# A two-layer encoder trunk on one core: when the attention layer's gated products are issued, and where two sums stand in their engines' order

## The chip, the core and the metric

The kernel runs on one core of a Trainium2 chip. The core has five engines that work side by side, each on its own list of instructions in a fixed order: TensorE (PE: matrix products and transposes into PSUM), VectorE (DVE), ScalarE (ACT), GpSimd (POOL) and SyncE (SP, here only a queue for DMAs). Engines wait for each other by semaphores, and an instruction that waits holds up everything behind it on its own engine. POOL's list holds DMAs too. The metric is the device time of one execution in microseconds.

## The reference, cut to what matters

512 tokens and 16 meta tokens (T = 528), width 2048, two layers. Layer 0 is grouped-query attention with 16 query heads in 8 groups of two, each group with one key and one value head; layer 1 is gated linear attention. For layer 0:

```python
proj = h @ w_in
q, k, v, gate = jnp.split(proj, ...)
q = apply_axial_rope(rmsnorm(q, q_norm), ang_row, ang_col)
k = apply_axial_rope(rmsnorm(k, k_norm), ang_row, ang_col)
s = jnp.einsum('bqkgd,bskd->bkgqs', qb, k) * (ATTN_HEAD_DIM ** -0.5)
p = jax.nn.softmax(s, axis=-1)
o = jnp.einsum('bkgqs,bskd->bqkgd', p, v)
return (o * jax.nn.silu(gate)) @ w_out
```

The change concerns the product `o * silu(gate)`, the mean of squares in `rmsnorm` of q and k, and how the large weight products (`h @ w_in`, `@ w_out`, and layer 1's `h @ w_in`) are formed.

## The kernel before, in words

**Numbers in two parts.** Every fp32 operand of a product is split into a high part, rounded by ACT (`A.copy`, line 132), and a rest, subtracted by DVE (line 133): `uh`, `ul` for activations, `whi`, `wlo` for weights (three buffers of each, used in turn). Each product is three matmuls: high by high, high by rest, rest by high.

**What sets the order.** The program is traced by Python. `Clock` (line 39) is the author's planner: each product step advances it by an estimated cost in microseconds, `clk.after(dt, fn)` puts work `dt` later, and `clk.drive` runs a generator that yields its own pauses. So the planner's due times decide in which order instructions are traced. A scheduler then builds each engine's list from priorities (`tc.high_priority(n)` moves work ahead) and from when it thinks the operands are there; work that seems ready can float ahead of what was traced before it. `pin` (`keep_in_program_order`) forbids that for one instruction: it stays behind the instruction traced last before it on the same engine. It adds no semaphore.

**The attention stage** (lines 796 to 818) goes through eight groups. In group g, PE runs the three projections of group g+1 (`qkv`: k, then two q heads), and between their steps the planner sets the attention of group g: nine tiles of queries, each with `softmax` (products L701 to L703 into `s`; maximum L706 on DVE; exponential L709 on ACT) and, one slot later, `transposed`: PE transposes the probabilities `pn` into PSUM tiles `pT` and `pTm` (L721, L723), ACT and DVE split them into `ph`, `pl`, `pmt` (L725 to L728). `pT` and `pTm` come from a PSUM pool of two buffers, so a tile's transposes must wait until the tile before has been split. The fifth tile holds the 16 meta tokens of both heads and is split in two halves, one for each head. A projection ends in `rope`: POOL sends four DMAs (L314) that swap rows, waits for them, and runs three tensor operations (`rotate`, L315 to L317); ACT and DVE split the squares, PE sums them with a matrix of ones (L328, L329), DVE scales (L331), ACT makes the inverse root (L136, L137), DVE multiplies (L335).

**The gated products** of the group before, two heads of each, run beside this in `stored_gates` (line 652). The gate values were stored earlier and are loaded by `load_gates`. `begin` scales them (L658, DVE) and forms SiLU (L140 to L142 on ACT, L689 on POOL); `inverse` loads the softmax denominators' inverses, spread over all partitions (L641, POOL's queue); `end` runs on POOL alone: `divided` (L645 and a narrow L646), the product with the attention output (L664) and its store (L665). By the planner: begin of head 0 at 7.0, its `inverse` at 9.2, begin of head 1 at 10.0, its `inverse` and the end of head 0 at 18.0, the end of head 1 at 21.2.

**The paired weight products**, `seven` (line 217), form two column blocks of a weight matrix in seven products instead of eight, from sums of the four quarter blocks a11, a12, a21, a22. It runs eight times ahead of the attention, four times in the output projection, and six times in layer 1's projection. In each run `parts` splits the weights of seven products in the order w1, w6, w2, s, a21, a11, a22, two products ahead of their use, as buffers come free; DVE forms four sums (L234). The first, s = a21 + a22, with priority 90, may be issued as soon as its two loads have landed.

Of the kernel before, what the change touches and what calls it, by code (L numbers as in the profile page):

```python
# [14 lines left out]
ALU = mybir.AluOpType  # L15
# [67 lines left out]
def hybrid_encoder(  # L83
# [6 lines left out]
    V, A, G, PE = nc.vector, nc.scalar, nc.gpsimd, nc.tensor  # L90
    clk = Clock()
    pin = tc.keep_in_program_order
# [26 lines left out]
    ones_r = const.tile([P, P], F32R, name="ones_r")  # L119
# [11 lines left out]
    def split(hi, lo, src):  # L131
        A.copy(hi, src)  # L132
        V.tensor_tensor(lo, src, hi.bitcast(F32), op=ALU.subtract)  # L133

    def rsqrt_inplace(t):
        A.activation(t, t, AF.Ln)  # L136
        A.activation(t, t, AF.Exp, scale=-0.5)  # L137
# [79 lines left out]
    def seven(src, c, ys, th, tl, free, ps_x):  # L217

        def quarter(t, i, j):
            with tc.high_priority(AHEAD + 200):  # L220
                nc.sync.dma_start(out=t.rearrange("p (k n) -> p k n", n=P),
                                  in_=src[:, j * KH:(j + 1) * KH, c + i * P:c + (i + 1) * P])
            return t

        def parts(raw):
            with tc.high_priority(AHEAD):
                hi = wpool.tile([P, 1024], F32R, tag="whi", name="whi")
                lo = wpool.tile([P, 1024], F32R, tag="wlo", name="wlo")
                split(hi, lo, raw)
            return [t.rearrange("p (k n) -> p k n", n=P) for t in (hi, lo)]  # L230

        def sums(o, a, b, op=ALU.subtract):
            with tc.high_priority(90):
                V.tensor_tensor(o, a, b, op=op)  # L234

        def product(w, b, ps=None, more=False):
            if ps is None:
                ps = ps_x.tile([P, 512], F32, tag="x", name="px")[:, :HALF]
            bh, bl = b
            for k in range(KH):  # L240
                PE.matmul(ps, w[0][:, k], bh[:, k], start=k == 0 and not more, stop=False, skip_group_check=more)  # L241
                PE.matmul(ps, w[0][:, k], bl[:, k], start=False, stop=False, skip_group_check=more)  # L242
                PE.matmul(ps, w[1][:, k], bh[:, k], start=False, stop=k == KH - 1,  # L243
                          skip_group_check=more)
                clk.step(3 * (HALF + 7) / 2400)
            return ps

        def add(o, ps, y):
            with tc.high_priority(AHEAD + 100):
                V.tensor_tensor(o, ps, y, op=ALU.add)  # L250

        def of_u(j, n):
            a, b = HALVES[n]
            return [t[:, j * KH:(j + 1) * KH, a:b] for t in (uh, ul)]

        def of_t(o):
            return [t[:, :, o:o + HALF] for t in (th, tl)]
        a11, a21, a22, s, a12, spare = free
        for t, i, j in ((a11, 0, 0), (a12, 0, 1), (a21, 1, 0), (a22, 1, 1)):
            quarter(t, i, j)  # L260
        y1, y2 = ys
        l, r = slice(0, HALF), slice(HALF, T)
        w1 = parts(a11)
        w6 = parts(a12)
        sums(s, a21, a22, ALU.add)
        sums(a21, a11, a21)
        sums(a11, s, a11)
        w2 = parts(a11)
        p1 = ps_p.tile([P, 512], F32, tag="pp", name="pp")[:, :HALF]
        product(w1, of_u(0, 0), p1)  # L270
        A.copy(y1[:, l], p1)
        add(y1[:, l], product(w6, of_u(1, 0)), y1[:, l])
        product(w2, of_t(T2), p1, True)
        A.copy(y1[:, r], p1)
        p5 = product(parts(s), of_t(T1))
        A.copy(y2[:, r], p5)
        sums(a11, a12, a11)
        product(parts(a21), of_t(T3), p1, True)
        A.copy(y2[:, l], p1)
        add(y2[:, r], y2[:, l], y2[:, r])  # L280
        product(parts(a11), of_u(1, 1), p5, True)
        add(y1[:, r], p5, y1[:, r])
        product(parts(a22), of_t(T4), p1, True)
        A.copy(y2[:, l], p1)
        return [spare, a21, a12, a11, s, a22]
# [33 lines left out]
    def rope(qw, sq, outs, steps):  # L319
        rotate(qw, wk.tile([P, T], F32, tag="qs", name="qs"))  # L320
        sh = wk.tile([P, T], F32R, tag="sh", name="sh", bufs=1)
        sl = wk.tile([P, T], F32R, tag="sl", name="sl", bufs=1)
        split(sh, sl, sq)
        f = sq

        def sums(a, b):
            ps = ps_p.tile([P, 512], F32, tag="pp", name="ssq")[:, :b - a]
            PE.matmul(ps, ones_r, sh[:, a:b], start=True, stop=False)  # L328
            PE.matmul(ps, ones_r, sl[:, a:b], start=False, stop=True)  # L329
            with tc.high_priority(AHEAD):  # L330
                V.scalar_tensor_tensor(f[:, a:b], ps, 1.0 / P, erow[:, a:b], op0=ALU.mult, op1=ALU.add)  # L331

        def late():
            rsqrt_inplace(f)
            V.tensor_tensor(qw, qw, f, op=ALU.mult)  # L335
            for hi, lo, a, b in outs:
                split(hi, lo, qw[:, a:b])
        for step, part in zip(steps, HALVES):
            clk.after(step, lambda part=part: sums(*part))
        clk.after(steps[2], late)  # L340
# [62 lines left out]
    for i, (si, off) in enumerate(((0, 0), (1, 0), (1, P))):  # L403
        for j, (a, b) in enumerate(HALVES):
            n = 2 * i + j
            if n < 3:
                ps = ps_p.tile([P, 512], F32, tag="pp", name="pp")
            else:
                ps = ps_g.tile([P, 512], F32, name=f"g{n}")
            ps = ps[:, :b - a]  # L410
# [140 lines left out]
    for h in range(3):  # L551
        y = yp.tile([P, T], F32, tag=f"y{h % 2}", name="y")
# [6 lines left out]
    y = yp.tile([P, T], F32, tag="y1", name="y")  # L559
# [91 lines left out]

    def stored_gates(hs, held):

        grs = ready.pop() if ready else load_gates(hs)
        gss = []

        def begin(i):
            pin(V.tensor_tensor(grs[i], grs[i], rrow, op=ALU.mult))  # L658
            gss.append(silu(grs[i]))

        def end(i):
            divided(gss[i], grs[i])
            og = held[hs[i] % 2]
            G.tensor_tensor(og, og, gss[i], op=ALU.mult)  # L664
            nc.gpsimd.dma_start(out=og_d[hs[i]], in_=og)  # L665
        yield 7.0
        for i, (x, y) in enumerate(((2.2, 0.8), (8.0, 0.0))[:len(hs)]):
            begin(i)
            yield x
            inverse(hs[i], grs[i])  # L670
            yield y
        for i in range(len(hs)):
            end(i)
            yield 3.2
        if hs and hs[-1] < 12:
            ready.append(load_gates([h for h in (hs[-1] + 1, hs[-1] + 2) if h < 13]))

    ready = []

    def load_gates(hs):  # L680
        grs = [wa.tile([P, T], F32, tag="gr", name="gr") for _ in hs]
        for gr, h in zip(grs, hs):
            pin(nc.gpsimd.dma_start(out=gr, in_=g_d[h]))
        return grs

    def silu(gr):
        gs = wa.tile([P, T], F32, tag="gs", name="gs", bufs=2)
        sigmoid(gs, gr)
        pin(G.tensor_tensor(gs, gs, gr, op=ALU.mult))  # L689
        return gs  # L690
# [102 lines left out]

    qk, vv = qks[0][0], values(0)
    held = None
    for g in range(KV):
        o_sb = o_tiles()
        if g == KV - 1:
            clk.after(10.5, make_sel)
        att = clk.drive(chain(iter([3.0]), attention(g, qk, vv, o_sb, SLOTS[g])))  # L800
        gates = [] if g == 0 else [2 * g - 2, 2 * g - 1]
        stored = clk.drive(stored_gates([h for h in gates if h < 13], held))
        if g + 1 < KV:
            nxt = qkv(g + 1)
        for h in gates:
            if h < 13:
                continue
            gs = gate(h)
            rb = wa.tile([P, T], F32, tag="gr", name="rb")
            inverse(h, rb)  # L810
            divided(gs, rb)
            og = held[h % 2]
            G.tensor_tensor(og, og, gs, op=ALU.mult)
            nc.gpsimd.dma_start(out=og_d[h], in_=og)
        if g + 1 < KV:
            clk.finish(att, stored)
            qk, vv = nxt
            held = o_sb
# [28 lines left out]
    for m in range(2):  # L847
        for j, (a, b) in enumerate(HALVES):
            ps = (ps_t.tile([P, 512], F32, tag="t", name="po") if m and j else
                  ps_p.tile([P, 512], F32, tag="pp", name="pp"))[:, :b - a]  # L850
# [42 lines left out]
    for m in range(2, 5):  # L893
        y = y_tile(m % 2)
# [19 lines left out]
    hs = [tp.tile([P, T], F32, name=f"h{k}") for k in range(KT)]  # L914
# [51 lines left out]
    for i in range(2):  # L966
        for a, b in HALVES:
            ps = ps_g.tile([P, 512], F32, name=f"g{i}{a}")[:, :b - a]
# [116 lines left out]
    for a, b in HALVES:  # L1085
        ps = ps_t.tile([P, 512], F32, tag="t", name="lrf")[:64, :b - a]
# [406 lines left out]
    y = [fp.tile([P, D], F32, name=f"y{t}") for t in range(4)]  # L1493
# [75 lines left out]
```

## Time and profile before

| | |
|---|---|
| Median of 3 runs | 1774.61 us (1770.96 to 1779.83) |
| The profiled execution | 1778.32 us, its span 1776.4 us |
| PE busy | 1737.5 us, 98% of the span |
| DVE, ACT, POOL busy | 1153.0, 1000.4, 386.9 us |
| Attention stage | about 297 to 750 us of the span |
| Runs of `seven` | about 116 to 286, 806 to 890, 1020 to 1150 us |

The span reaches from the first to the last instruction. PE's granted clock was 0.999 of full speed. A row of the timeline has the start in us from the beginning of the span, the duration in us, engine, line, operation, written tile <- read tiles, and in brackets how long the engine sat idle before, and for whom. In a table of waits, a row has who waited for whom, the total in us, how often, and the longest.

### The profile page before, as it was taken

How to read it: one execution, taken by the hardware profiler on the slowest of the kernel's cores; microseconds unless marked ns; L12 is line 12 of the kernel's file. 1: busy time of each engine (PE TensorE's matmuls, PEld its weight loads, DVE VectorE, ACT ScalarE, POOL GpSimd, SP SyncE). 2: the span in 40 equal slices, each digit the busy share in tenths (PEclk: the TensorE clock that was granted, in tenths of full speed). 3: DMA queues.
4: the chain of work that ended last, by engine and by line, in shares of the span. 5: the costliest groups of instructions: out<-in, count | busy, mean ns of one | idle time of the engine just before them, and what ended most of it. 6: DMA issues, size and time to landing. Idle time of an engine off the chain costs nothing.

```text
span 1776.4 us, 31587 instructions
## 1 busy us (share of the span) xinstructions
PE 1737.5 (98%) x12427; PEld 1635.0 (92%) x12427; DVE 1153.0 (65%) x1791; ACT 1000.4 (56%) x2056; POOL 386.9 (22%) x492
## 2 busy tenths in 40 slices
PE   8999999999999999999999999999999999999998
PEld 8999999999999999999999899998898989888886
DVE  5767875566566666786766976567685865863224
ACT  5545445666666666644457454577684765853222
POOL 3103301356456645231141001110100000000000
PEclk9999999999999999999999999999999999999999
DMA  7444434233333334464485344343342432344323
GB/s 244 142 133 132 130 118 125 79 110 109 85 106 103 107 85 127 133 200 119 121 249 173 104 135 120 110 136 90 87 111 73 114 87 86 107 141 174 95 95 130
DMA packets 272387, 218.80 MB, mean 123 GB/s; under 512 B 13196, under 2 KB 243280, under 8 KB 271712
## 3 DMA queue, kind: packets, MB, share of 16 engines
q1 hardware_dynamic: 253200, 157.41, 31.4%
q0 software_dynamic: 19040, 59.40, 10.1%
q8 instruction: 97, 1.59, 0.4%
q14 instruction: 50, 0.41, 0.1%
HBM read 176.83 MB, written 33.44 MB: 118 GB/s over the span
## 4 chain that ended last, share of the span: by engine, by line
PE 77%; issue 7%; DVE 7%; ACT 5%; DMA 2%; POOL 2%; SPq 0%; DVEq 0%; POOLq 0%; ACTq 0%
PE pp L155 12%; PE pp L157 12%; PE pp L156 12%; PE pp L241 3%; PE pp L242 3%; PE pp L243 3%; PE f L1481 2%; PE f L1479 2%; PE f L1480 2%; PE px L243 2%; PE px L241 2%; PE px L242 2%; DVE wlo L133 2%; ACT whi L132 2%; PE pT L721 1%
## 5 line engine op out<-in xcount | busy, mean ns | idle before, releaser
L155 PE MATMUL pp<-uh,whi 128*128 128x264 f32 (+1 forms) x1872 | 585.4, 313 | 0.7 <-ACT y L888 0.5
L157 PE MATMUL pp<-uh,wlo 128*128 128x264 f32 (+1 forms) x1872 | 576.3, 308 | 1.4 <-DVE wlo L133 1.1
L156 PE MATMUL pp<-ul,whi 128*128 128x264 f32 (+1 forms) x1872 | 575.3, 307 | 0.0
L133 DVE TENSOR_TENSOR wlo<-wraw,whi 128x1024 fp32r<-128x1024 f32 (+1 forms) x226 | 287.9, 1274 | 238.4 <-ACT whi L132 237.9
L132 ACT CAST whi<-wraw 128x1024 fp32r<-128x1024 f32 (+1 forms) x226 | 235.4, 1042 | 261.3 <-PE f L1481 83.4
L157 PEld LDWEIGHTS pp<-uh,wlo 128*128 128x128 f32 x1872 | 353.4, 189 | 18.8 <-DVE wlo L133 1.6
L155 PEld LDWEIGHTS pp<-uh,whi 128*128 128x128 f32 x1872 | 353.4, 189 | 16.9 <-ACT y L888 0.7
L156 PEld LDWEIGHTS pp<-ul,whi 128*128 128x128 f32 x1872 | 353.8, 189 | 13.5
L132 ACT CAST whi<-x 128x1024 fp32r<-128x1024 f32 x72 | 75.5, 1049 | 104.9 <-PE pp L242 52.1
L133 DVE TENSOR_TENSOR wlo<-x,whi 128x1024 fp32r<-128x1024 f32 x72 | 90.2, 1260 | 40.0 <-ACT whi L132 39.7
L709 ACT ACTIVATE pn<-s,mx 128x528 f32<-128x528 f32 (+1 forms) x72 | 50.5, 701 | 71.3 <-DVE mx L706 71.3
L706 DVE TENSOR_REDUCE mx<-s 128x1 f32<-128x528 f32 (+1 forms) x72 | 50.8, 706 | 52.8 <-PE s L703 52.3
L243 PE MATMUL px<-uh,wlo 128*128 128x264 f32 x288 | 82.0, 285 | 0.8 <-DVE wlo L133 0.8
L241 PE MATMUL px<-uh,whi 128*128 128x264 f32 x288 | 82.2, 285 | 0.4 <-ACT whi L132 0.4
L242 PE MATMUL px<-ul,whi 128*128 128x264 f32 x288 | 81.5, 283 | 0.0
L1481 PE MATMUL f<-whi,ul 128*128 128x512 f32 x192 | 75.6, 394 | 0.0
L1479 PE MATMUL f<-whi,uh 128*128 128x512 f32 x192 | 75.5, 393 | 0.0
L1480 PE MATMUL f<-wlo,uh 128*128 128x512 f32 x192 | 75.3, 392 | 0.0
L314 POOL DMA_DIRECT2D qs<-qw x96 | 48.0, 506 | 95.1 <-ACT sq L308 72.9
L726 DVE TENSOR_TENSOR pl<-pT,ph 128x512 fp32r<-128x512 f32 (+1 forms) x80 | 47.6, 595 | 26.7 <-ACT ph L725 26.2
L243 PE MATMUL pp<-t0h,wlo 128*128 128x264 f32 x192 | 54.4, 283 | 2.1 <-DVE wlo L133 2.1
L243 PEld LDWEIGHTS px<-uh,wlo 128*128 128x128 f32 x288 | 54.1, 188 | 1.0 <-DVE wlo L133 1.0
(488 smaller groups left out, 4433.9 us busy)
## 6 DMA issues: line engine op xcount, KB each, us to landing
wraw<-in_gla_w_in_dram SPq DMA_DIRECT2D x82, 512.0 KB, 3.9
wraw<-in_attn_w_in_dram SPq DMA_DIRECT2D x75, 512.0 KB, 4.0
wraw<-in_gla_w_out_dram SPq DMA_DIRECT2D x32, 512.0 KB, 3.9
wraw<-in_attn_w_out_dram SPq DMA_DIRECT2D x23, 512.0 KB, 4.5
x<-in_attn_w_in_dram SPq DMA_DIRECT2D x19, 512.0 KB, 4.4
x<-in_gla_w_in_dram SPq DMA_DIRECT2D x14, 512.0 KB, 4.5
qs<-qw POOLq DMA_DIRECT2D x96, 66.0 KB, 3.3
g_d<-y POOLq DMA_DIRECT2D x20, 264.0 KB, 2.4
```

What stands on the lines that cost most here:

```text
L132: A.copy(hi, src)
L133: V.tensor_tensor(lo, src, hi.bitcast(F32), op=ALU.subtract)
L155: PE.matmul(ps, wh, uh[:, k, a:b], start=first, stop=False)
L156: PE.matmul(ps, wh, ul[:, k, a:b], start=False, stop=False)
L157: PE.matmul(ps, wl, uh[:, k, a:b], start=False, stop=last)
L241: PE.matmul(ps, w[0][:, k], bh[:, k], start=k == 0 and not more, stop=False, skip_group_check=more)
L242: PE.matmul(ps, w[0][:, k], bl[:, k], start=False, stop=False, skip_group_check=more)
L243: PE.matmul(ps, w[1][:, k], bh[:, k], start=False, stop=k == KH - 1, skip_group_check=more)
L706: V.reduce_max(mx, s, axis=AX.XY, negate=True)
L1479: PE.matmul(ps, uh[:, k, ts], wh[:, kk], start=(k == 0), stop=False)
L1480: PE.matmul(ps, uh[:, k, ts], wl[:, kk], start=False, stop=False)
L1481: PE.matmul(ps, ul[:, k, ts], wh[:, kk], start=False, stop=(k == KT - 1))
```

## The change

It has four edits. In `stored_gates` the due times become: begin of head 0 at 3.8, `inverse` at 6.4, end of head 0 at 9.2, begin of head 1 at 15.6, its `inverse` at 17.8, its end at 29.8, and then the load of the next two gates. The first two gates are loaded in group 0, 20.0 after its start, not at the start of group 1. In `rope`, the first of the two matmuls of each sum of squares is pinned. In `seven`, the sum s is pinned, and the instruction traced before it on DVE is the subtraction for w6.

```diff
@@ seven
         def sums(o, a, b, op=ALU.subtract):
             with tc.high_priority(90):
-                V.tensor_tensor(o, a, b, op=op)
+                return V.tensor_tensor(o, a, b, op=op)
...
         w1 = parts(a11)
         w6 = parts(a12)
-        sums(s, a21, a22, ALU.add)
+        pin(sums(s, a21, a22, ALU.add))
         sums(a21, a11, a21)
         sums(a11, s, a11)
         w2 = parts(a11)
@@ rope
-            PE.matmul(ps, ones_r, sh[:, a:b], start=True, stop=False)
+            pin(PE.matmul(ps, ones_r, sh[:, a:b], start=True, stop=False))
             PE.matmul(ps, ones_r, sl[:, a:b], start=False, stop=True)
@@ stored_gates
-        grs = ready.pop() if ready else load_gates(hs)
+        grs = ready.pop() if hs else []
...
-        yield 7.0
-        for i, (x, y) in enumerate(((2.2, 0.8), (8.0, 0.0))[:len(hs)]):
+        yield 3.8
+        for i, (x, y, z) in enumerate(((2.6, 2.8, 6.4), (2.2, 12.0, 0.0))[:len(hs)]):
             begin(i)
             yield x
             inverse(hs[i], grs[i])
             yield y
-        for i in range(len(hs)):
             end(i)
-            yield 3.2
+            yield z
         if hs and hs[-1] < 12:
             ready.append(load_gates([h for h in (hs[-1] + 1, hs[-1] + 2) if h < 13]))
@@ main loop
     held = None
+    clk.after(20.0, lambda: ready.append(load_gates([0, 1])))
     for g in range(KV):
```

## The prediction, made before the changed kernel was run

> **What bounds the kernel now.** The page comes first, then the table of what PE waited for.
>
> ```profile
> span 1776.4 us, 31587 instructions
> ...
> PE 1737.5 (98%) x12427; PEld 1635.0 (92%) x12427; DVE 1153.0 (65%) x1791; ACT 1000.4 (56%) x2056; POOL 386.9 (22%) x492
> ```
> ```profile
> PE pT L721 <- DVE pl L726: 12.4, 7, 2.5
> ...
> PE pp L243 <- DVE wlo L133: 2.1, 1, 2.1
> PE ssq L328 <- ACT sh L132: 1.9, 7, 0.7
> ...
> PE px L243 <- DVE wlo L133: 0.8, 1, 0.8
> ...
> PE px L241 <- ACT whi L132: 0.4, 1, 0.4
> ```
>
> PE bounds the kernel. The change adds and removes no matmul, so it can only close or open PE's gaps, 1776.4 - 1737.5 = 38.9 us at most, start and end included. Each edit has its row here: the gated products 12.4, the sums of squares 1.9, the sum in `seven` 2.1 + 0.8 + 0.4 = 3.3; 17.6 us in all. Six of the seven `pT` gaps are one in each of groups 1 to 6, behind the meta tile; I look at the longest. POOL, DVE and PE in that stretch:
>
> ```profile
> 606.12 1.55 POOL L645 TENSOR_TENSOR gs<-gs,gr 128x512 f32<-128x512 f32 x1
> 607.74 2.19 POOL L664 TENSOR_TENSOR o_sb<-o_sb,gs 128x528 f32<-128x528 f32 x1
> ...
> 610.84 1.57 POOL L645 TENSOR_TENSOR gs<-gs,gr 128x512 f32<-128x512 f32 x1
> ...
> 613.65 1.30 POOL L664 TENSOR_TENSOR o_sb<-o_sb,gs 128x528 f32<-128x528 f32 x1
> ```
> ```profile
> 605.96 2.80 DVE L133 TENSOR_TENSOR wlo<-wraw,whi 128x1024 fp32r<-128x1024 f32 x1 [0.54 <-ACT whi L132]
> ...
> 611.83 1.67 DVE L133 TENSOR_TENSOR wlo<-wraw,whi 128x1024 fp32r<-128x1024 f32 x1 [1.30 <-ACT whi L132]
> ...
> 613.87 1.65 DVE L335 TENSOR_TENSOR qw<-qw,sq 128x528 f32<-128x528 f32 x1
> 615.55 0.23 DVE L726 TENSOR_TENSOR pl<-pT,ph 128x64 fp32r<-128x64 f32 x1
> ```
> ```profile
> 615.92 0.63 PE L721 MATMUL pT<-ident,pn 128*128 128x128 f32 x4 [2.46 <-DVE pl L726]
> ```
> ```profile
> L335 DVE TENSOR_TENSOR qw<-qw,sq x21: 707/709/1662, 323.7 to 703.7; 128x528 f32<-128x528 f32 x21
> ```
>
> From 606 to 615 POOL works through both heads' products, and what DVE does on SBUF operands beside it is stretched: L335 takes 1.65 us against a least of 0.71, and the two weight splits 2.80 and 1.67 against the 1.21 of a row below. The maximum and the splits of the meta tile stand behind them on DVE, and PE stands for 2.46 us until the last `pl`. DVE is not full (65%); it is late there.
>
> **The gated products.** The same instructions stay: per head L658, three ACT steps, L689, one load, L645, L646, L664, one store, and a load of the next gate; nothing is added on any queue. Stretched time in front of that `pl`: (2.80 - 1.21) + (1.67 - 1.21) + (1.65 - 0.71) = 3.0 us, more than the gap of 2.46. With the first head's products moved from 18.0 to 9.2 and the second's from 21.2 to 29.8, none stands beside the meta tile, which the planner splits at about 21.2; so the gap goes, in all six groups. The seventh gap is in group 7:
>
> ```profile
> 708.92 0.63 PE L721 MATMUL pT<-ident,pn 128*128 128x128 f32 x4 [1.71 <-DVE pl L726]
> ```
>
> No projection of q and k runs there, and I leave it. Gain 12.4 - 1.7 = 10.7.
>
> What is late next? The first head's products now come between tiles two and three, ahead of the k head's rotation, and there PE has little to spare:
>
> ```profile
> 477.34 0.64 ACT L142 ACTIVATE gs<-gs 128x528 f32<-128x528 f32 x1
> ...
> 478.40 0.59 ACT L725 CAST ph<-pT 128x512 fp32r<-128x512 f32 x1
> ```
> ```profile
> 479.23 0.68 DVE L726 TENSOR_TENSOR pl<-pT,ph 128x512 fp32r<-128x512 f32 x1
> ```
> ```profile
> 480.07 0.63 PE L721 MATMUL pT<-ident,pn 128*128 128x128 f32 x4
> ```
>
> `pl` ends at 479.91 and PE's transposes start 0.16 later. But what made this `pl` late is ACT: the second head's sigmoid (L140 to L142, three steps of 0.64) ends just ahead of `ph`, and the change takes it away from there (10.0 to 15.6), some 1.9 us of ACT. Against that, 1.55 + 1.3 us of POOL work may stretch one or two DVE splits by about 1.3 each. The load ahead of L645 makes POOL wait, but the four DMAs of the rotation behind it need a projection that ends later. I take 0.25 us of new gaps in each of six groups, 1.5 in all (bounds 0, and 2.6 in each, or 15.6), nearer to the low end, because the sigmoid's 1.9 covers one stretched split. The second head's products go behind the next rotation, beside tiles six to eight, where none of the seven gaps lies now; they are in the same bounds. The earlier load of the first gates costs nothing: POOL has nothing else then. **Term: -10.7 + 1.5 = -9.2.**
>
> **The sums of squares.** The pin lets the seven short waits on `sh` fall behind matmuls that are ready: -1.9. On the other side L331 and the inverse root come some matmuls later; as a bound I take the row's total turned round, +1.9. What the pinned matmul waits for is ready by then, so the low end is nearer. **Term: -1.9.**
>
> **The sum in `seven`.** DVE and PE around the gap of 2.1, ahead of the attention:
>
> ```profile
> 175.31 1.23 DVE L234 TENSOR_TENSOR x<-wraw 128x1024 f32<-128x1024 f32 x1 [3.03 <-DMA wraw<-in_attn_w_in_dram]
> 176.57 2.23 DVE L234 TENSOR_TENSOR wraw<-x,wraw 128x1024 f32<-128x1024 f32 x1
> 178.73 4.59 DVE L133 TENSOR_TENSOR wlo<-x,whi 128x1024 fp32r<-128x1024 f32 x2
> ```
> ```profile
> 181.11 0.39 PE L243 MATMUL pp<-t0h,wlo 128*128 128x264 f32 x1 [2.13 <-DVE wlo L133]
> ```
>
> DVE stood 3.03 us for the load of s, with the split of the run before (a22) behind it, and PE needed that split 2.13 before 181.11. With s behind w6 the split is done first: -2.1. But the three sums now come late. The same place in the output projection's second run:
>
> ```profile
> 826.90 1.05 ACT L132 CAST whi<-x 128x1024 fp32r<-128x1024 f32 x1 [1.59 <-PE px L242]
> ```
> ```profile
> 828.37 1.21 DVE L133 TENSOR_TENSOR wlo<-x,whi 128x1024 fp32r<-128x1024 f32 x1
> ...
> 832.20 2.30 DVE L234 TENSOR_TENSOR xs<-x,xs 128x1024 f32<-128x1024 f32 x1
> ```
> ```profile
> 829.34 1.44 POOL L882 TENSOR_TENSOR acc<-acc,sq 128x528 f32<-128x528 f32 x1
> ...
> 832.07 1.33 POOL L882 TENSOR_TENSOR acc<-acc,sq 128x528 f32<-128x528 f32 x1
> ```
> ```profile
> 835.79 0.28 PE L243 MATMUL pp<-sh,wlo 128*128 128x264 f32 x1
> ```
>
> The cast for w6 waits for PE to free a buffer, so s can't start before 826.90 + 1.05 + 1.21 + 0.1 = 829.26. Then s, a21, a11 (1.23 each and 0.03 between) to 833.0, the cast of w2 1.05 to 834.1, its split 1.21 to 835.35. PE used w2's rest at 835.79: 0.4 us to spare where POOL is quiet. POOL is not quiet: after each run but the first it has two adds (L882). The 2.30 of the row at 832.20 is 1.33 of such an add, less 0.13, and the sum's own 1.1: one waits for the other entirely. With both adds (1.3 each) between the three sums, 835.35 becomes some 837.7, so PE stands for 837.7 - 835.79 = 1.9. Three runs: +5.7.
>
> The Trainium skill ("SBUF — State Buffer", section "SBUF: two separate sides") speaks against the edit here: VectorE instructions with two SBUF inputs and GpSimd instructions that read SBUF take a shared pair of ports for their whole length, and the other blocks fully. The rows at 832 agree; read as mere slowing by half, without that rule, the three runs would lose about 2.
>
> In the attention's second run it is the rotation that stands in that place:
>
> ```profile
> 140.11 1.45 POOL L315 TENSOR_TENSOR qw<-qw,cos 128x528 f32<-128x528 f32 x1
> ...
> 143.91 2.20 POOL L317 TENSOR_TENSOR qw<-qw,qs 128x528 f32<-128x528 f32 x1
> ```
>
> Three operations from 140.1 to 146.1, beside sums that would run from 139.8: by the same working PE stands for about 2.0 there, and 0.4 in another run, where `first_group` has short DVE steps. In layer 1's first run w6 is loaded late:
>
> ```profile
> 1014.07 1.22 DVE L234 TENSOR_TENSOR x<-wraw,x 128x1024 f32<-128x1024 f32 x1
> ...
> 1016.38 1.22 DVE L234 TENSOR_TENSOR wraw<-wraw 128x1024 f32<-128x1024 f32 x1
> ```
> ```profile
> 1022.79 1.05 ACT L132 CAST whi<-x 128x1024 fp32r<-128x1024 f32 x1 [7.53 <-DMA x<-in_gla_w_in_dram]
> ```
> ```profile
> 1028.18 0.28 PE L243 MATMUL pp<-th,wlo 128*128 128x264 f32 x1
> ```
>
> The same chain, 8.4 us from that cast (826.90 to 835.35 above), ends at 1031.2, against the 1028.18 at which PE used w2's rest: +3.0. But DVE, without two sums of 1.22 in front of the work that frees the load's buffer, may let it start 2.4 earlier: +0.6, which I round up to 0.8. The other runs of layer 1 have no POOL arithmetic: 0. **Term: -2.1 + 5.7 + 2.0 + 0.4 + 0.8 = +6.8** (bounds: -3.3, its whole row; +14, if each of 17 runs also lost the 0.4 of spare).
>
> Sum: -9.2 - 1.9 + 6.8 = -4.3. The profiled execution, 1778.32 (span 1776.4 and 1.9 around it), would be 1774.0. It lay 3.7 above the median of the three runs, within their range; taken from the median 1774.61, the forecast is **1770.3**.
>
> **The rivals.**
> *The sums hide after all.* If adds and sums miss each other, or PE's lead over the splits is greater than worked out, the last edit only gains: 1774.6 - 9.2 - 1.9 - 2.1 = 1761.4. For it: by the table of waits, 16 of the 18 runs have no gap, and splits are made two products ahead. Against it: the cast at 826.90 is released by PE itself (px L242), so the chain behind it can't start earlier. 0.28.
> *Slower: the first head's products stop tiles two and three.* If the 2.8 us of POOL work stretches two splits in front of that `pl`, by 1.3 each, and ACT's freed time doesn't reach it, six groups open 2.6: 15.6 in place of the 10.7 closed. 1774.6 + 4.9 - 1.9 + 6.8 = 1784.4. It decides from about 1 us of new gap in a group, where with the third edit the gain is gone. For it: 0.16 us to spare at 480.07. Against: ACT's sigmoid leaves. 0.12.
> *The gap behind the meta tile doesn't go.* `pT` has two buffers and the meta tile is split in two rounds between ACT and DVE; if that exchange alone takes the time, moving POOL's work changes nothing: 1774.6 - 1.9 + 6.8 = 1779.5. The stretched 3.0 us in front of it speak against. The Trainium skill ("Perfetto Trace Analysis", section "Optimization Strategy") reads a gap that repeats as a possible lack of SBUF or PSUM for the next tile, which would be this case. 0.15.
>
> **How the numbers follow.** Forecast 0.45, rivals 0.28, 0.12, 0.15. A measurement of this kernel tells about 0.5% (8.9 us) from no change: below 1765.7 is faster, above 1783.5 slower. Faster: most of the first rival and a little of the forecast, 0.29. Slower: two thirds of the second and a little of the third, 0.10. Within: 0.61. The range, 1760 to 1781, takes in the first rival but for its low edge and the third whole, and leaves out the second.
>
> **What would show it.** Right: the row `pT` <- `pl` falls from 12.4 to about 3; `ssq` <- `sh` is gone; new rows of PE waiting for w2's casts and splits, about 1.9 each in three runs of the output projection and 2.0 in the attention's second run, with sums of over 2 us. Wrong: gaps at tiles two and three of a group; no gap at w2; the meta tile's gap still there with L335 at 0.71.

## The result, and the profile after

| | before | after |
|---|---|---|
| Median of 12 runs each | 1775.72 us (1770.96 to 1780.97) | 1783.72 us (1780.78 to 1790.31) |
| The profiled execution, its span | 1778.32 us, 1776.4 us | 1782.52 us, 1780.8 us |
| PE busy in that execution | 1737.5 us | 1739.9 us |

The ratio of after to before is 1.0037, with a 95% interval of 1.0023 to 1.0052: the changed kernel is some 4 to 9 us slower. The prediction had it 4.3 us faster, and its range ended at 1781. The two profiled executions lie 4.2 apart, at the low end of the interval, because the one of before was above its median and the one of after below. Where the text below goes by stages, it goes by these two.

The page of after, its span and its busy times (engine, busy us, share, instructions):

```profile
span 1780.8 us, 31566 instructions
...
PE 1739.9 (98%) x12427; PEld 1635.4 (92%) x12427; DVE 1154.0 (65%) x1791; ACT 999.7 (56%) x2056; POOL 389.1 (22%) x492
```

PE still bounds the kernel and has the same 12427 matmuls. The gaps between them moved. The table of what PE waited for, after (who <- whom: total us, times, longest; L720 and L725 are lines 721 and 726 of before):

```profile
PE pp L241 <- ACT y L271: 9.1, 5, 2.7
PE pT L720 <- DVE vl L617: 3.0, 4, 0.9
PE pp L156 <- DVE ul L446: 2.7, 1, 2.7
...
PE ssq L328 <- ACT sh L132: 2.1, 7, 0.6
...
PE pT L720 <- DVE pl L725: 1.3, 1, 1.3
```

Each edit has its row. `pT` <- `pl` fell from 12.4 in seven waits to 1.3 in one: the gated products did what they were moved for. `ssq` <- `sh` is 2.1 where it was 1.9: the pin of the squares did nothing. `pp` <- `y` L271 is new, 9.1 in five waits: PE stands before the third product of a run of `seven`, that of w2, which goes on adding in the PSUM buffer that the copy at L271 reads out. Two of these waits are in the attention's projections and three in the output projection. And `pT` <- `vl` is new in the attention, where `pTm` <- `vl`, 1.0 in one wait before, is gone.

To see which stage lost what, I use the first and the last matmul on the rests of weights (L243) of each kind of run. The view by line, before and then after: number, duration in ns, start of the first and of the last in us:

```profile
L243 PE MATMUL pp<-sh,wlo x96: 280/283/285, 815.4 to 890.9; 128*128 128x264 f32 x96
L243 PE MATMUL px<-t0h,wlo x64: 281/286/288, 128.5 to 277.6; 128*128 128x264 f32 x64
L243 PE MATMUL px<-th,wlo x48: 278/285/288, 1031.1 to 1141.2; 128*128 128x264 f32 x48
```
```profile
L243 PE MATMUL pp<-sh,wlo x96: 279/283/285, 812.8 to 894.0; 128*128 128x264 f32 x96
L243 PE MATMUL px<-t0h,wlo x64: 280/286/288, 129.4 to 282.5; 128*128 128x264 f32 x64
L243 PE MATMUL px<-th,wlo x48: 279/284/288, 1035.5 to 1145.5; 128*128 128x264 f32 x48
```

| stretch | before | after | difference | predicted |
|---|---|---|---|---|
| up to the first `px<-t0h` | 128.5 | 129.4 | +0.9 | 0 |
| attention's projections (`px<-t0h`) | 149.1 | 153.1 | +4.0 | -2.1 + 2.0 + 0.4 = +0.3 |
| from there to the first `pp<-sh`: the attention | 537.8 | 530.3 | -7.5 | -9.2 - 1.9 = -11.1 |
| output projection (`pp<-sh`) | 75.5 | 81.2 | +5.7 | +5.7 |
| from there through layer 1's projections to the end | 885.5 | 886.8 | +1.3 | +0.8 |
| sum | 1776.4 | 1780.8 | +4.4 | -4.3 |

The output projection came out to the tenth, the attention's projections missed by 3.7, and the attention by 3.6. The first row is not the change: DVE waits 3.69 us there for a load of the input, which arrives at other times from run to run. The gap that it leaves on PE (`pp` <- `ul`) was nothing in the profile of before and 2.7 in this one; of the experiments below it was nothing in `seven_no_rotation`, which has the third edit, and 2.6 in `later_and_a22_again`, which has another pin. Behind it PE ran at half clock from 31.4 to 34.8 us after. The stretch of the row lies between 126.6 and 129.4 us in all 13 profiles, in no order by edit.

This is the attention's second run of seven after the change (start, us, engine, line, operation, written <- read, idle before):

```profile
140.30 1.62 POOL L315 TENSOR_TENSOR qw<-qw,cos 128x528 f32<-128x528 f32 x1 [0.46 <-DMA qs<-qw]
140.65 2.35 DVE L234 TENSOR_TENSOR wraw<-wraw,x 128x1024 f32<-128x1024 f32 x1
...
141.90 2.29 POOL L316 TENSOR_TENSOR qs<-qs,sin 128x528 f32<-128x528 f32 x1
143.04 2.23 DVE L234 TENSOR_TENSOR wraw<-x,wraw 128x1024 f32<-128x1024 f32 x1
144.26 2.20 POOL L317 TENSOR_TENSOR qw<-qw,qs 128x528 f32<-128x528 f32 x1
145.30 2.24 DVE L234 TENSOR_TENSOR x<-wraw,x 128x1024 f32<-128x1024 f32 x1
...
147.57 1.04 ACT L132 CAST whi<-x 128x1024 fp32r<-128x1024 f32 x1 [5.75 <-DVE x L234]
148.53 1.04 ACT L132 CAST whi<-wraw 128x1024 fp32r<-128x1024 f32 x1
...
149.47 0.37 ACT L271 COPY y<-pp 128x264 f32<-128x264 f32 x1
```
```profile
149.90 0.39 PE L241 MATMUL pp<-t0h,whi 128*128 128x264 f32 x1 [2.67 <-ACT y L271]
```

DVE's three sums and POOL's three operations of the rotation stand in a chain, each sum over 2.2 us where a quiet one takes 1.23. So the cast of w2 starts at 147.57 only. The releaser that the table names, the copy at L271, is just the last of three things on ACT behind the late sum. In the third run it is the first sum that meets the rotation:

```profile
187.22 2.34 DVE L234 TENSOR_TENSOR x<-wraw 128x1024 f32<-128x1024 f32 x1
```
```profile
194.44 0.39 PE L241 MATMUL pp<-t0h,whi 128*128 128x264 f32 x1 [1.48 <-ACT y L271]
```

In the output projection it is POOL's adds of squares (L882) that two of the sums meet. POOL and DVE of its second run, then PE:

```profile
826.07 1.75 POOL L882 TENSOR_TENSOR acc<-acc,sq 128x528 f32<-128x528 f32 x1 [0.33 <-ACT sq L881]
826.55 2.35 DVE L234 TENSOR_TENSOR wraw<-wraw,xs 128x1024 f32<-128x1024 f32 x1
...
828.67 1.41 POOL L882 TENSOR_TENSOR acc<-acc,sq 128x528 f32<-128x528 f32 x1
828.93 2.23 DVE L234 TENSOR_TENSOR wraw<-xs,wraw 128x1024 f32<-128x1024 f32 x1
```
```profile
832.85 0.28 PE L243 MATMUL px<-uh,wlo 128*128 128x264 f32 x1
834.78 0.39 PE L241 MATMUL pp<-sh,whi 128*128 128x264 f32 x1 [1.65 <-ACT y L271]
835.00 0.28 PE L242 MATMUL pp<-sl,whi 128*128 128x264 f32 x1
```

Matmuls of this size start 0.12 us apart where nothing is late. From 832.85 to 835.00 are two such steps, so a gap of 1.65 costs PE 2.15 - 0.24 = 1.91 us: a gap counts only from the end of the matmul before it.

### The profile page after: what moved, and what is told of

It reads as the page before. It is cut to its first block, busy times and chain, and to the rows that moved or that the text cites. A ratio compares the mean times of both kernels' runs of the same rounds, so it can differ in the third digit from the quotient of the medians.

```text
span 1780.8 us, 31566 instructions
## 1 busy us (share of the span) xinstructions
PE 1739.9 (98%) x12427; PEld 1635.4 (92%) x12427; DVE 1154.0 (65%) x1791; ACT 999.7 (56%) x2056; POOL 389.1 (22%) x492
## 5 line engine op out<-in xcount | busy, mean ns | idle before, releaser
L133 DVE TENSOR_TENSOR wlo<-wraw,whi 128x1024 fp32r<-128x1024 f32 (+1 forms) x226 | 284.0, 1257 | 240.8 <-ACT whi L132 239.5
L243 PE MATMUL px<-uh,wlo 128*128 128x264 f32 x288 | 81.9, 285 | 0.0
L241 PE MATMUL pp<-t0h,whi 128*128 128x264 f32 x192 | 55.7, 290 | 4.2 <-ACT y L271 4.1
L725 DVE TENSOR_TENSOR pl<-pT,ph 128x512 fp32r<-128x512 f32 (+1 forms) x80 | 47.5, 594 | 18.1 <-ACT ph L724 17.4
L242 PE MATMUL pp<-t0l,whi 128*128 128x264 f32 x192 | 55.4, 289 | 0.0
```

## The experiments

The kernel before ran beside each group: 1776.42 us beside `gates_only`, `seven_only`, `seven_no_adds` and `pin_behind_w1`; 1776.69 beside `products_later`, `pin_behind_a22`, `later_and_a22` and `seven_no_rotation`; 1776.58 beside `squares_only`, `later_and_a22_again` and `products_later_again`.

**One edit at a time.** `gates_only` is the first edit alone (the due times of `stored_gates` and the earlier load of the first gates), `squares_only` the second, `seven_only` the third, each as in the diff above.

> The changed due times of the gated products alone (the pin of the squares changes no engine's order and is left out, the sum in seven is as before). Theory: the loss of the change sits in the pinned sum and the gates' edit gains what the attention stage shows in the profile after, 7.6 us: 1775.7 - 7.6 = 1768 (1765 to 1771), the six gaps of 0.8 to 2.5 before the transposes behind the meta tile gone, gaps of 0.6 to 0.9 at the first tile of a group in their place. Rival: the gates' edit costs elsewhere what it gains: 1775 or more.

> The change's second edit alone, the first product of the sums of squares held to its emitted place. Theory (it changes nothing: TensorE already took these products in the emitted order, and the gaps ahead of them are the wait for ScalarE's copy of the squares, which a place in the order doesn't shorten): a ratio to the kernel before of 0.999 to 1.001, and the row of waits of ssq for sh at about 2.1 us in 7 waits as before. Rival (the author's term: the products stood behind others, and the pin takes 1.9 us off): 1774.5 or less where the kernel before takes 1776.4, and that row under 0.5.

> The pinned sum in seven alone. Theory: it costs what the stages with seven lost in the profile after, 4.2 + 5.9 + 1.2 = 11.3 us: 1787 (1784 to 1790), with gaps before w2 of about 2.7 and 1.5 ahead of the attention and three of 1.65 in the output projection, and the attention's gaps as before; where a gap comes near 2.7, a stretch of 3.4 us at half clock behind it. Rival: the loss comes only with the gates' edit: 1778 or less.

| kernel | median | ratio to before, 95% interval |
|---|---|---|
| `gates_only` | 1771.94 us | 0.9968 (0.9954 to 0.9981) |
| `squares_only` | 1775.45 us | 0.9996 (0.9986 to 1.0005) |
| `seven_only` | 1788.01 us | 1.0066 (1.0047 to 1.0085) |

The first came out 0.9 above the expected 1765 to 1771, the third 1.0 above its 1787. The product of the three is 1.0030, against 1.0037 for the whole change: within the intervals, the edits add. The loss is the third edit's, and it outweighs the first edit's gain of 4.5 us about two and a half times. The table of waits of `squares_only`:

```profile
PE ssq L328 <- ACT sh L132: 1.6, 7, 0.4
```

Seven waits on `sh` as before. All five engines take their instructions in the same order with this pin as without it, so there was nothing to move.

**What makes the sums late.** Two kernels on top of `seven_only`, each with one of the POOL operations that run beside the sums left out:

```diff
@@ seven_no_adds: the sums of squares of the output projection, from block 5 on
-            G.tensor_tensor(acc[:, a:b], acc[:, a:b], sq, op=ALU.add)
+            if m < 5:
+                G.tensor_tensor(acc[:, a:b], acc[:, a:b], sq, op=ALU.add)
@@ seven_no_rotation: the first group's rotation (first_group calls it with whole=False)
-        G.tensor_tensor(qw, qw, cos, op=ALU.mult)
-        G.tensor_tensor(qs, qs, sin, op=ALU.mult)
-        G.tensor_tensor(qw, qw, qs, op=ALU.add)
+        if whole:
+            G.tensor_tensor(qw, qw, cos, op=ALU.mult)
+            G.tensor_tensor(qs, qs, sin, op=ALU.mult)
+            G.tensor_tensor(qw, qw, qs, op=ALU.add)
```

> The pinned sum in seven alone, and POOL's adds of squares (acc + sq) left out in the output projection from the sixth column block on, so that the norm behind it misses most squares; nothing else is changed. Theory (sums and adds exclude each other on SBUF): the three gaps of 1.65 before w2 in the output projection go, and no sum there takes over 1.3 us; the two gaps ahead of the attention stay; about 5 us less than with the adds. Rival (the chain behind w6 is too long by itself): the three gaps stay at 1 us or more.

> The change's third edit alone (it took 1788.0), and the three POOL operations that rotate the first group's queries and keys left out; this part of the computation is missing. Theory (in the attention's second and third run the sums share their time with these POOL operations, and are late by them): the gaps of 2.67 at 146.0 and 1.48 at 191.7 fall below 0.5, and with the first also the stretch of half clock of about 1.5 us behind it: 1782 to 1785. Rival (the late product waits for ScalarE, whose copy of a projection stands behind two casts of weights, and the casts are late because the pinned sums start late, POOL or not): the gap at 146 stays at 1 us or more, and the time at 1786 or more.

The view by line of L243, `seven_only`, then `seven_no_adds`, then `seven_no_rotation`:

```profile
L243 PE MATMUL pp<-sh,wlo x96: 280/283/287, 814.1 to 895.3; 128*128 128x264 f32 x96
L243 PE MATMUL px<-t0h,wlo x64: 281/286/288, 128.2 to 281.2; 128*128 128x264 f32 x64
```
```profile
L243 PE MATMUL pp<-sh,wlo x96: 280/283/285, 815.0 to 890.5; 128*128 128x264 f32 x96
L243 PE MATMUL px<-t0h,wlo x64: 281/286/288, 126.6 to 278.3; 128*128 128x264 f32 x64
```
```profile
L243 PE MATMUL pp<-sh,wlo x96: 280/283/290, 813.3 to 894.5; 128*128 128x264 f32 x96
L243 PE MATMUL px<-t0h,wlo x64: 281/286/288, 128.4 to 275.3; 128*128 128x264 f32 x64
```

Without the adds the output projection is back from 81.2 to 75.5 us, what it took before the change; without the rotation it stays at 81.2, and the attention's projections go from 153.0 to 146.9, 2.2 less than before the change. Where the POOL operations are gone, no gap stands at the runs' third products, and the sums have their quiet length. From `seven_no_adds`, and below it from `seven_no_rotation` the table of waits:

```profile
828.73 1.22 DVE L234 TENSOR_TENSOR wraw<-wraw,xs 128x1024 f32<-128x1024 f32 x1
...
829.99 1.23 DVE L234 TENSOR_TENSOR wraw<-xs,wraw 128x1024 f32<-128x1024 f32 x1
```
```profile
PE pp L241 <- ACT y L271: 5.0, 3, 1.7
```

The five waits of after are three here: those of the output projection, where the adds remain. The rival, that ACT's queue delays the product whatever POOL does, falls: the two casts and the copy are still there, and the gaps are gone. The times don't settle it. Without the rotation it is 1784.4 us (ratio 1.0052, 1.0032 to 1.0071), within the expected 1782 to 1785, but the interval overlaps that of `seven_only`. Without the adds it is 1787.91 (1.0061, 1.004 to 1.0082), no less than `seven_only`, where 5 less was expected. By the profiles its attention took 3.8 us more than that of `seven_only` (536.7 against 532.9 between the two groups of L243) and the way from the output projection to the first `px<-th` 3.8 more (146.5 against 142.7), and with four runs the intervals are too wide for 5 us; in each of the two PE ran at half clock once (at 617 and 1033 us; the last section has what that costs), which `seven_only` doesn't have there, and the rest stays open. The stages with the POOL work show the cause; the time alone wouldn't.

**Where the pin may stand.** Two kernels with the first edit and the sum s pinned earlier: `pin_behind_w1` between the splits of the pair (this one also with the second edit), `pin_behind_a22` ahead of both, right behind the last split of the run before.

```diff
@@ pin_behind_w1
         w1 = parts(a11)
+        pin(sums(s, a21, a22, ALU.add))
         w6 = parts(a12)
-        sums(s, a21, a22, ALU.add)
@@ pin_behind_a22
+        pin(sums(s, a21, a22, ALU.add))
         w1 = parts(a11)
         w6 = parts(a12)
-        sums(s, a21, a22, ALU.add)
```

> The whole change, but the sum s is traced and pinned between the splits of w1 and w6, not behind both. Theory: the sum then doesn't wait for the buffer that PE frees for w6, so the gaps before w2 shrink to 0.3 or less, and the old gap of 2.1 behind a waiting sum is gone too: 1764 to 1768. Rival: any pin of s puts three sums in a row behind the release: gaps before w2 of 1 us or more remain, 1775 or more.

> The first edit, and the first sum of weights of a run of seven products held to the place where it is emitted ahead of the split of its first weight, which is right behind the last split of the run before, in place of behind the pair. Theory (a pin costs only where it makes the sums late against the product that uses them; here they start 2.4 us earlier than with the change's pin): no gap over 0.5 ahead of a run's second product anywhere, the 2.1 gap of the third run of the attention's projections gone or under 0.8, and 1769 to 1771 against 1771.9 for the first edit alone. Rival (any pin of that sum makes another split late, since VectorE then has three sums of 1.2 us in front of the split of the first weight): gaps of 1 us or more at the first products of the runs, and 1774 or more.

| kernel | median, ratio | attention's projections | output projection |
|---|---|---|---|
| after (behind both splits) | 1783.72, 1.0037 | 153.1 | 81.2 |
| `pin_behind_w1` | 1772.73, 0.9981 (0.9968 to 0.9995) | 149.3 | 77.5 |
| `pin_behind_a22` | 1772.49, 0.9975 (0.9959 to 0.9991) | 147.5 | 75.5 |
| `gates_only` (no pin) | 1771.94, 0.9968 (0.9954 to 0.9981) | 148.7 | 75.5 |

`pin_behind_w1` was expected at 1764 to 1768 with gaps of 0.3 at most; its gaps ahead of the third products were 0.4 to 1.34, together 3.0 where the change had 9.1, so a third of the waiting is still there. The same pin costs 5.7 us in the output projection behind two splits, 2.0 behind one and nothing behind none. Behind none it also takes away most of what the third edit was aimed at: the wait `pp` L243 <- `wlo` of `pin_behind_a22` is 0.5, where before had 2.1, and the projections are 1.6 us shorter than with no pin before the change (149.1) and 1.2 shorter than `gates_only`. In the time of the whole kernel that doesn't show: 1769 to 1771 was expected, 1772.49 measured, and nothing tells it from `gates_only`.

**What remains of the first edit's gain.** In `gates_only` the attention's seven gaps behind the meta tile are one, but new waits are there. The table of waits, and one group's third tile:

```profile
PE s L700 <- ACT pn L708: 3.9, 4, 1.1
...
PE pT L720 <- DVE pl L725: 2.1, 1, 2.1
```
```profile
470.37 1.55 POOL L645 TENSOR_TENSOR gs<-gs,gr 128x512 f32<-128x512 f32 x1 [3.14 <-DMA gr<-r_d]
470.40 2.17 DVE L133 TENSOR_TENSOR ql<-qw,qh 128x512 fp32r<-128x512 f32 x2
...
472.61 0.71 DVE L705 TENSOR_REDUCE mx<-s 128x1 f32<-128x528 f32 x1
472.62 1.30 POOL L664 TENSOR_TENSOR o_sb<-o_sb,gs 128x528 f32<-128x528 f32 x1
473.23 1.78 DVE L133 TENSOR_TENSOR wlo<-wraw,whi 128x1024 fp32r<-128x1024 f32 x1
473.35 0.70 ACT L708 ACTIVATE pn<-s,mx 128x528 f32<-128x528 f32 x1 [1.80 <-DVE mx L705]
```
```profile
474.19 0.39 PE L700 MATMUL s<-kh,qh 128*128 128x264 f32 x1 [1.02 <-ACT pn L708]
```

Beside the first head's product at L645 one of the two splits `ql` in the row of 2.17 us takes 2.06, where none takes over 0.71 once the product stands elsewhere (below); the maximum stands behind it on DVE, ACT waits 1.80 for the maximum, and PE 1.02 for the exponential. So `products_later` moves the end of the first head 3.2 units later, to behind the rotation of the next keys on POOL:

```diff
-        for i, (x, y, z) in enumerate(((2.6, 2.8, 6.4), (2.2, 12.0, 0.0))[:len(hs)]):
+        for i, (x, y, z) in enumerate(((2.6, 6.0, 3.2), (2.2, 12.0, 0.0))[:len(hs)]):
```

> The change's first edit alone, with the first head's product issued 3.2 of the author's clock units later (its end set at 6.0 in place of 2.8 after its inverse), so that on POOL it comes behind the rotation of the next keys. Theory (the new gaps of about 1.0 us ahead of each group's third tile come from the first head's product on POOL, which stretches the VectorE splits there from 0.7 to 2.1 and makes the exponential late): those gaps fall below 0.4 in at least four of the six groups and the gap behind the meta tile stays away, so about 4 us less than the edit alone at 1771.9: 1766 to 1769. Rival (whatever POOL does in that stretch costs the same, since its total of work per group is unchanged): the gaps only move to another tile, the sum of the gaps in the attention stays within 1.5 of 8.9, and the time stays at 1771 to 1774.

> The kernel with the later first product alone, for the comparison with the one before: 1765 to 1768.

It took 1766.87 us (0.9948, 0.9931 to 0.9965), and 1768.89 (0.9950, 0.9938 to 0.9963) in the other group, 0.9 above what was expected there. The split `ql`, by line, in `gates_only` and then in `products_later` (count: shortest/median/longest in ns):

```profile
L133 DVE TENSOR_TENSOR ql<-qw,qh x24: 159/708/2061, 287.5 to 699.3; 128x528 fp32r<-128x528 f32 x8, 128x512 fp32r<-128x512 f32 x8, 128x16 fp32r<-128x16 f32 x8
```
```profile
L133 DVE TENSOR_TENSOR ql<-qw,qh x24: 163/692/712, 288.6 to 694.1; 128x528 fp32r<-128x528 f32 x8, 128x512 fp32r<-128x512 f32 x8, 128x16 fp32r<-128x16 f32 x8
```

None is stretched any more, and the wait of `s` for `pn` is gone from the table. The rival (the gaps only move) falls. By stages, from the last `px<-t0h` to the first `pp<-sh`, the attention took

| due times of the gates | profiles | attention, us |
|---|---|---|
| old | before, `squares_only`, and the three on `seven_only` | 532.9 to 538.0 |
| of the change | after, `gates_only`, both earlier pins | 529.1 to 532.5 |
| first head's end 3.2 later | four profiles | 524.0 to 525.5 |

so the change's due times and the later product are each worth between 5 and 6 us there (means of 536.2, 530.7 and 525.0).

**Both together.** `later_and_a22` has the later product and the pin ahead of both splits; it was run twice, the second time beside `products_later` again.

> The later first product and the earlier pin in one kernel. Theory (both work and touch different stages, so they add): 1764 to 1768, faster than either alone. Rival (one of the two brings nothing): the time of the better of the two alone, within 1.5.

> The kernel with the later first product and the earlier pin once more, beside the one with the later product alone, to tell whether the third run's gap of 2.0, which the pin takes away, is worth its time. Theory (a gap of TensorE is lost time wherever it stands): 1.5 to 2 below the kernel with the later product alone. Rival (the gap is given back behind it, where TensorE waits less by as much): the same time within 0.7.

It took 1767.24 us (0.9950, 0.9931 to 0.9968) and 1767.76 (0.9948, 0.9936 to 0.9961), against 1766.87 and 1768.89 for the later product alone: 0.4 slower and 1.1 faster. So the pair isn't shown to be faster than the later product alone, and 1.1 lies between what theory and rival said of the second time. The pin's gain is there in its stage (147.5 and 147.7 us against 149.8 and 149.2), and layer 1 gives it back: from the last `pp<-sh` to the first `px<-th` the two profiles took 146.2 and 144.4 us against 140.2 and 142.6, and `pin_behind_a22` 144.2 against 142.3 in `gates_only`. The seven kernels with s pinned ahead of both splits or behind both have three gaps in layer 1's first run, of 1.03 to 1.07, 0.45 or 0.46, and 0.43 or 0.44 us; the other six don't have them. Not all of the 6.0 of the first pair is the pin's: its profile also has a wait of 1.76 at 891 us for a cast of other weights. Either kernel beats both that were compared, by about 0.5% against before. Of the two, `products_later` has the smaller edit.

## Why the prediction was wrong

**The gated products: the mechanism right, one term too small.** It said that the gap behind the meta tile goes in six groups, 10.7 us in all; the row fell by 11.1. It allowed 1.5 for new gaps, 0.25 a group, because ACT's sigmoid leaves and "covers one stretched split". The new rows after are 3.0 (`vl`) and 1.1 (`s` <- `pn`), together 4.1, with 1.0 of `pTm` <- `vl` gone; in `gates_only` they were 3.9 (`pn`) and 1.3 (`vl`). The cover was on the wrong engine: what is late at the third tile is the maximum on DVE, behind the stretched `ql`, and ACT stands idle 1.80 us for it, so freed time on ACT buys nothing. This is the slower rival's mechanism, at 1 us in four groups rather than 2.6 in six. `products_later` shows it for the waits on `pn`. For the waits on `vl` the traces have a likely cause, which no run tests: the first head's sigmoid (L140 to L142), due at 3.8 and no longer at 7.0, now stands on ACT among the splits of the values (L616) in each of these groups, at 469.3 to 471.5 of the group whose splits start at 469.8, where before none stood among them. So while the second head's sigmoid left one place on ACT, the first head's came to another, which the prediction left out. Why the waits are 3.0 after and 1.3 in `gates_only`, with the same order there, stays open. That the measured 1783.72 lies beside this rival's 1784.4 is a coincidence: the attention gained 7.5 us, where the rival has it losing.

**The sums of squares: no term at all.** The step that failed is "the pin lets the seven short waits on `sh` fall behind matmuls that are ready". The pin holds an order, and the order was already that one. The question to ask first was whether another matmul stood between in the timeline of before. Predicted -1.9, measured a ratio of 0.9996.

**The sum in `seven`.** The working of the output projection held in the main: cast, split, three sums and two adds of POOL that can't overlap gave 1.9 a run and 5.7 in all. PE stood 1.65 three times, which costs it 1.91 each, and the stage is 5.7 longer. That it fits to the tenth is luck. From the cast for w6 to the end of the sums the working has 8.45 us (833.0 and 2.35 more, less 826.90), and it took 8.09 (824.33 to 832.42); and it lets PE wait for w2's split alone, where PE stood for the copy at L271 behind two casts on ACT, so that w2's rest was used 2.70 behind the sums and not 2.35. The two errors cancel. The Trainium skill ("SBUF — State Buffer", section "SBUF: two separate sides") has VectorE with two SBUF inputs and GpSimd lock each other out for a whole instruction; the 5.7, against the 2 of a mere slowing, agrees.

The attention's projections failed, +4.0 for +0.3, in three places.
- The third run was booked as -2.1, its gap of 2.13 gone, and nothing set against it. The rotation stands in this run as well, between 183.2 and 188.5, beside a split and the first sum, which take 2.00 and 2.34 us. PE stands 1.48: the old wait went, a new one came, and the gain was 0.65. Without the rotation there is no gap (`seven_no_rotation`).
- The second run was booked at 2.0 "by the same working", which has two POOL operations; there are three, each sum meets one, and PE stood 2.67, which by the starts of its matmuls (146.95 to 150.12, less 0.24) costs 2.93.
- Behind that gap PE ran at half its clock for 3.4 us, which nothing in the prediction priced. The rows by windows are below; it cost about 1.5.

Together 0.65 taken from 2.93 + 1.5 is +3.8, nearly all of the 4.0. The 0.4 booked for another run didn't come: no gap over 0.3 stands there. Layer 1 was booked as +0.8 and the stretch behind the output projection took 1.3.

**The rivals.** "The sums hide after all" had the highest chance of them and is excluded by the two kernels on `seven_only`. Its argument, that 16 of 18 runs had no gap, counted runs in which the sums started earlier and said nothing of runs where they start behind two splits. "The gap behind the meta tile doesn't go" is excluded by its row. That the forecast's sum came out 8.7 too low against its own profile needed no rival: it is 3.7 of the projections, 1.7 + 1.9 of the attention's two terms, 0.5 of layer 1, and 0.9 of the start.

## What to carry to other kernels

When an edit moves instructions of one engine behind others, list what the other engines do in the whole stretch where they now fall, in every run of the loop, the run included whose gap the edit removes. An engine's freed time covers a new delay only if that engine is the one that the waiting matmul is late by: follow the chain back before crediting it. And a pin has a price by where it stands: three places for the same sum cost 5.7, 2.0 and 0 us in one stage, and the last of them lost in another stage what it gained in a third.

## What the runs showed of the hardware

PE's granted clock falls to half behind some gaps of under 3 us. Windows of after at 147 to 155 us (window, length, busy of each engine with instructions, granted clock, DMA share, GB/s), and the same window of before:

```profile
150.40:150.90 0.50, 0.50 (x7) 0.50 (x6) 0.50 (x1) 0.40 (x1) 0.00 (x0) 0.99 0.00 0
150.90:154.30 3.40, 3.40 (x17) 3.40 (x17) 3.34 (x5) 0.00 (x0) 0.00 (x0) 0.50 0.61 167
154.30:155.00 0.70, 0.70 (x8) 0.70 (x7) 0.00 (x0) 0.43 (x1) 0.00 (x0) 1.00 0.69 166
```
```profile
150.90:154.30 3.40, 3.40 (x30) 3.40 (x29) 1.59 (x2) 1.55 (x3) 0.00 (x0) 1.00 0.59 170
```

17 matmuls start in the 3.4 us where 30 did before: 13 of 0.12 us each are lost, about 1.5. It began 1.0 us after PE had resumed from the gap of 2.67, and lasted 3.4 us. The Trainium skill ("TensorE: Matmul & The Clock Gate", section "Part 1: The HAM clock gate (the "warmup" mystery)") puts the half clock after an idle window of about 3.4 us; here 2.67 were enough. The size of the gap doesn't decide it alone: a gap of 2.67 at 144.39 us in `seven_no_adds` and one of 2.46 at 613.46 in before had no such stretch behind them, while in `gates_only` one of 2.07 at 698.06 had.

Where the gap lies decides too. In all 13 traces every change of the clock behind its first rise to full lies a whole number of steps of 3.413 us from that rise: in `gates_only` the rise is at 14.92, and the changes at 701.00, 704.41, 1018.44 and 1021.85 are 201, 202, 294 and 295 steps behind it. Divide each trace into windows by these steps, and compare PE's busy time in them. The gap of 2.67 after lies almost whole in one window and leaves it 0.99 busy; in `seven_no_adds` a border at 146.06 divides the same gap in two, and leaves 1.75 and 2.41:

```profile
147.48:150.89 3.41, 0.99 (x8) 1.00 (x9) 2.30 (x3) 3.22 (x4) 0.00 (x0) 1.00 0.22 79
```
```profile
142.64:146.06 3.42, 1.75 (x15) 1.54 (x13) 2.31 (x2) 1.32 (x2) 1.51 (x2) 1.00 0.22 79
146.06:149.47 3.41, 2.41 (x19) 2.41 (x20) 3.41 (x4) 1.89 (x3) 0.00 (x0) 1.00 0.05 14
```

The traces have some 6640 such windows between the first rise and the kernel's end. Each of the 11 in which PE was busy for less than 1.58 us was followed by one window of half clock, none of those over 2.02 us was, and of the 36 between 7 were; what decides among these stays open. The borders stand anywhere against the kernel's start: the first rise lies 0.1 to 3.3 us behind a whole number of steps. Windows that run free of the kernel, as the same section has them, fit that. So a gap of 2 to 3 us on PE may cost 1.5 us more than its size, and whether it does depends on where a border falls, which differs from place to place and from run to run.
